# State-space outputs and gate kept as channels by tokens, the skip as a per-partition scalar, and the norm's root applied to the rows of the output projection

## The chip, the cores and the metric

The kernel runs on one core of a Trainium2 chip. The metric is the device time of one execution, in microseconds. Five engines work side by side, each through its own queue in order: PE (TensorE, matrix products into PSUM), DVE (VectorE), ACT (ScalarE), POOL (GpSimd) and SP (SyncE, which here issues the DMA transfers). PEld is the loading of a product's stationary operand.

## What is computed

One inference step of a one-layer trunk: 1024 prompt tokens and 8 streams of 16 decode tokens, width 1024. Three token mixers read the same normalised input: stick-breaking attention, a Mamba-2 state-space group (SSD) and forgetting attention (FoX). Cross-attention and a SwiGLU network follow. The change lies in the state-space group and in the projection that merges the three:

```python
proj = jnp.einsum('bnd,de->bne', u, p['w_in'])
sq, sk, sv, fq, fk, fv, fg, z, xbc, dt = split_last(proj, IN_SIZES)
...
xbc_c = jax.nn.silu(causal_dwconv(xbc_pad, p['conv_w'], p['conv_b']))
xs, Bm, Cm = split_last(xbc_c, (SSD_INNER, ...))
dt = jax.nn.softplus((dt + p['dt_bias']).astype(jnp.float32))
y, h_final = ssd_scan(xs * dt[..., None], dt * A, Bm, Cm, h0, ssd_chunk)
y = (y + p['d_skip'].astype(jnp.float32)[:, None] * xs).reshape(b, n, SSD_INNER)
ssd_o = rmsnorm(y * jax.nn.silu(z), p['ssd_norm_g'])      # over 512 channels
mix = jnp.concatenate([sb_o, fox_o, ssd_o], axis=-1)
out = jnp.einsum('bne,ed->bnd', mix, p['w_out'])
```

With y * silu(z) = s, the norm is s * g / sqrt(mean(s^2) + eps): the gain g belongs to a channel, the root to a token.

## The kernel before

All 1152 tokens stand in 9 blocks of 128; block 8 is the decode tokens. The normalised input is kept as channels by tokens (`uc`, three pieces of 384 tokens), each value as a high and a low part, so that a product of full precision is three products (`mm3`, lines 328 to 330).

**Two forms of projection.** `dense_T` keeps a weight tile stationary and streams 384 tokens: the result is 128 channels by 384 tokens. `dense_N` keeps 128 tokens stationary and streams up to 264 weight columns: the result is 128 tokens by channels. The convolution channels (`xbc_job`) come from `dense_T`, the gate (`z_proj`, `consume_z`) from `dense_N`, 256 columns at a time, with the 8 columns of dt beside its first half.

**The scan.** `ssd_gen` goes through the blocks in the order 8, 0, 1, ... 7, one chunk of 128 tokens each. For a chunk `load` fetches three things: the convolved channels, the decays broadcast to all partitions, and the gate. `prepare` transposes x and B to tokens by channels and makes the scaled forms of x (by dt, by the decay to the end, by the skip); `weights` makes the 128 by 128 decay weights of 8 heads; `states` multiplies C with the state (and for the decode block the streams' own states); `outputs` adds the heads' products, gates, squares with a sum over the row, and scales by the root and the gain; `write` transposes the 128 x 512 result to channels by tokens and stores it in `mix_sc`. The write of a chunk comes one chunk later, the last one in the `final` list.

**The order of the work.** A generator yields after each such step. The rows of both attentions are the main line; before each, the `fill` generator is advanced at the rate `RATE`: first the remaining projections in the order `ORD` (gate half 0, dt, convolution, gate half 1), then the scan. What is left is woven with the first half of the output projection (`heads_out`, `add_rows`: the attention channels), which adds 18 blocks of 128 x 512 into the residual rows `h`. Then `finish_rows` adds the state-space channels, again 18 products, from `mix_sc` by way of `load_unsplit`, which splits each value into high and low parts. The final place of each instruction on its engine is set by a scheduler that knows priorities and dependences.

**Buffers.** The scan's products take the 2 PSUM buffers `psd`, which the projections use too; the chunk's tiles A and B come from 6 big buffers `act`. DMA goes through SP's queue in order: a transfer that must wait for something holds all that is behind it.

Of the kernel before, what the change touches and what calls it, by code (L numbers as in the profile page):

```python
# [8 lines left out]
F32 = mybir.dt.float32  # L9
# [44 lines left out]
RATE = (1.0, 1.1, 60)  # L54
# [8 lines left out]
def tile_hybrid_step(ctx: ExitStack, tc: tile.TileContext, a: dict):  # L63
# [80 lines left out]
    SP.dma_start(out=rows[40:72, :P], in_=a["conv_w"][0].rearrange("i (k p) -> (i k) p", p=P))  # L144
    first_raw = []
# [73 lines left out]
    PE.transpose(colp[:, :72], rows[:72, :P], ident[:72, :72])  # L219
    cols = cst.tile([P, 72], F32, name="cols")  # L220
    DVE.tensor_copy(cols, colp[:, :72])
    DVE.tensor_scalar(cols[:, 32:72], cols[:, 32:72], 0.5, None, ALU.mult)
# [262 lines left out]
    def proj_v(m, c0, pv, sv, extra=0):  # L485
# [7 lines left out]
        return dense_N([(w_in, c0, 256 + extra)], blocks_of(uc), consume)  # L493
# [243 lines left out]
    def xbc_job(j):  # L737
# [9 lines left out]
        def consume(c, ps):  # L747
# [27 lines left out]
            SP.dma_start(out=xbc_sc[j * P:(j + 1) * P, 0:SEQ], in_=y)  # L775
            SP.dma_start(out=xbc_sc[j * P:(j + 1) * P, SEQ:T], in_=ysm[:, :P])
# [190 lines left out]
    def ssd_gen():  # L967
        sc = act_t(F32)
        hT, gB = sc[:, 0:512], sc[:, 512:1024]
# [65 lines left out]
        def load(i):  # L1035
            A = act_t(F32)
            SP.dma_start(out=A[:, 0:1024].rearrange("p (j t) -> p j t", t=P),
                         in_=xbc_sc[:, i * P:(i + 1) * P].rearrange("(j p) t -> p j t", p=P))
            SP.dma_start(out=A[:, 1024:2048],
                         in_=ac_sc[8 * i:8 * i + 8, :].rearrange("h t -> (h t)").unsqueeze(0).to_broadcast([P, 1024]))  # L1040
            SP.dma_start(out=A[:, 2048:2560], in_=z_sc[i * P:(i + 1) * P, :])
            return A

        def views(A, B):
# [4 lines left out]
        def prepare(i, A, B):
            xT, br, zt, Bn, cb, xn, xd, xe, xD = views(A, B)  # L1050
# [11 lines left out]
            heads_tt(xD, xn, ndsk)  # L1062

        def weights(i, A, B):
            xT, br, zt, Bn, cb, xn, xd, xe, xD = views(A, B)

            ps = pd()
            for g in range(2):
# [19 lines left out]
        def states(i, A, B, t1):  # L1088
            xT, br, zt, Bn, cb, xn, xd, xe, xD = views(A, B)
            hs = slice(8 * i, 8 * i + 8)  # L1090
            if i < 8:
                ps = pd()
                for g in range(2):
                    PE.matmul(ps[:, g * 256:(g + 1) * 256], xT[:, 6 + g, :], hT[:, g * 256:(g + 1) * 256],
                              start=True, stop=True)
                DVE.tensor_tensor(out=h3(t1), in0=h3(ps), in1=bc(ea[:, hs]), op=ALU.mult)
# [68 lines left out]
        def write(i, t1):  # L1165
            ps = pd()
            for j in range(4):
                PE.transpose(ps[:, j * P:(j + 1) * P], t1[:, j * P:(j + 1) * P], ident)
# [897 lines left out]
```

## Time and profile before

| | us |
|---|---|
| median of 3 runs | 1887.22 (1886.44 to 1888.09) |
| profiled execution | 1894.55 |
| its span, first to last instruction | 1892.8 |
| PE busy | 1837.7 (97%) |
| DVE busy | 886.4 (47%) |
| ACT busy | 802.1 (42%) |
| POOL busy | 617.9 (33%) |
| DMA, q1's share of 16 engines | 49.6% |

Lines of the page and of the trace name the line of the kernel, the engine, the operation and the tiles (output<-inputs), and how often. Busy times of matmuls overlap, so what a matmul costs PE is read from the distance between starts in the timeline. In brackets stands how long an engine was idle before an instruction and what released it; "issue" is idle time that nothing in the profile explains. Granted clock 1.00 is TensorE's full speed.

### The profile page before, as it was taken

The page shows a single profiled execution, that of the slowest core. Times are in us where ns is not written, and L with a number is a line of the kernel's source. Part 1 is how long each engine was busy: PE and PEld are TensorE (multiplying, and loading weights), DVE is VectorE, ACT ScalarE, POOL GpSimd, SP SyncE. Part 2 cuts the span into 40 slices and gives each one's busy share as a digit, 9 for nine tenths or more (in the row PEclk, how much of TensorE's full clock was granted, in tenths as well). Part 3 has the DMA queues.
Part 4 walks back from the last instruction along what each step waited for, and adds up shares of the span by engine and source line. Part 5 has one row for each costly group of instructions (what it writes and reads, how often), then busy time and mean ns, then how long its engine had stood idle before and what let it go on. Part 6 is the DMA issues. An engine that isn't in the chain of part 4 may idle for free.

```text
span 1892.8 us, 32368 instructions
## 1 busy us (share of the span) xinstructions
PE 1837.7 (97%) x12136; PEld 1638.6 (87%) x12136; DVE 886.4 (47%) x1798; ACT 802.1 (42%) x1719; POOL 617.9 (33%) x921
## 2 busy tenths in 40 slices
PE   7999999999999989999999989999999999999998
PEld 5899778888967767899988889999999999888886
DVE  3412323475656863444444586333333333455554
ACT  6522544545455862344332374333333333344443
POOL 7622425445115673111112107444444542000000
PEclk9999999999989999999999999999999999999999
DMA  9465654437587883245576124233322223657572
GB/s 338 145 189 149 206 142 133 147 109 207 179 249 228 282 290 102 108 134 173 173 271 219 56 81 112 75 87 79 76 71 70 70 70 105 207 187 243 174 243 89
DMA packets 291068, 296.64 MB, mean 157 GB/s; under 512 B 80092, under 2 KB 242884, under 8 KB 290912
## 3 DMA queue, kind: packets, MB, share of 16 engines
q1 hardware_dynamic: 290912, 294.57, 49.6%
q8 instruction: 96, 1.57, 0.3%
q14 instruction: 60, 0.49, 0.1%
HBM read 225.12 MB, written 69.91 MB: 156 GB/s over the span
## 4 chain that ended last, share of the span: by engine, by line
PE 83%; DMA 5%; DVE 4%; POOL 3%; ACT 3%; issue 2%; SPq 0%; DVEq 0%; POOLq 0%; ACTq 0%
PE psd L1868 11%; PE psd L328 10%; PE psd L329 10%; PE psd L330 10%; PE pst L1868 8%; PE pss L1868 4%; PE pss L328 3%; PE pss L330 3%; PE pss L329 3%; PE pso L1868 2%; POOL wl L132 2%; PE pst L328 1%; PE pst L329 1%; PE pst L330 1%; PE pso L593 1%
## 5 line engine op out<-in xcount | busy, mean ns | idle before, releaser
L132 POOL TENSOR_TENSOR wl<-wr,wh 128x256 fp32r<-128x256 f32 (+2 forms) x184 | 142.1, 805 | 233.0 <-ACT wh L292 232.8
L328 PE MATMUL psd<-act,wh 128*128 128x384 f32 x528 | 182.3, 345 | 0.0
L330 PE MATMUL psd<-act,wl 128*128 128x384 f32 x528 | 181.1, 343 | 0.6 <-POOL wl L132 0.6
L329 PE MATMUL psd<-act,wh 128*128 128x384 f32 x528 | 181.7, 344 | 0.0
L1868 PE MATMUL pst<-bT,tr 128*128 128x256 f32 (+1 forms) x1068 | 155.0, 293 | 0.0
L1868 PEld LDWEIGHTS pst<-bT,tr 128*128 128x128 f32 x1068 | 144.9, 188 | 0.1
L330 PE MATMUL psd<-wh,act 128*128 128x512 f32 (+3 forms) x424 | 136.9, 324 | 0.0
L329 PE MATMUL psd<-wl,act 128*128 128x256 f32 (+3 forms) x414 | 134.2, 325 | 2.7 <-POOL wl L132 2.7
L328 PE MATMUL psd<-wh,act 128*128 128x256 f32 (+3 forms) x414 | 133.3, 326 | 1.4 <-DMA act<-osc 1.0
L1868 PE MATMUL psd<-bT,tr 128*128 128x320 f32 (+1 forms) x912 | 132.8, 295 | 0.7 <-POOL tr L132 0.7
L1868 PEld LDWEIGHTS psd<-bT,tr 128*128 128x128 f32 x912 | 124.7, 188 | 1.0 <-POOL tr L132 0.9
L132 POOL TENSOR_TENSOR tr<-u,tr 128x256 fp32r<-128x256 f32 x110 | 82.6, 779 | 101.7 <-ACT tr L1704 83.8
L253 POOL TENSOR_SCALAR sm<-sm 128x1 f32<-128x1 f32 (+2 forms) x27 | 9.1, 338 | 297.3 <-ACT y L1970 207.8
L1843 DVE TENSOR_TENSOR tr<-tr,pst 128x256 f32<-128x256 f32 (+1 forms) x86 | 38.6, 449 | 139.9 <-ACT tr L1840 106.6
L330 PEld LDWEIGHTS psd<-act,wl 128*128 128x128 f32 x528 | 99.2, 188 | 3.2 <-issue 1.9
L132 POOL TENSOR_TENSOR ws<-ws 128x256 f32<-128x256 f32 (+2 forms) x100 | 69.3, 721 | 98.1 <-DVE ws L522 83.9
L328 PEld LDWEIGHTS psd<-act,wh 128*128 128x128 f32 x528 | 99.4, 188 | 2.2 <-issue 1.8
L329 PEld LDWEIGHTS psd<-act,wh 128*128 128x128 f32 x528 | 99.3, 188 | 1.9 <-issue 1.5
L132 POOL TENSOR_TENSOR tr<-raw,tr 128x256 fp32r<-128x256 f32 x94 | 69.2, 765 | 83.9 <-ACT tr L1704 75.7
L1704 ACT CAST tr<-tr 128x384 fp32r<-128x384 f32 (+1 forms) x70 | 37.6, 538 | 123.0 <-DMA tr<-hidsc 117.3
L329 PEld LDWEIGHTS psd<-wl,act 128*128 128x128 f32 x414 | 79.2, 191 | 10.9 <-POOL wl L132 4.0
L292 ACT CAST wh<-wr 128x512 fp32r<-128x512 f32 (+2 forms) x90 | 52.5, 622 | 81.7 <-PE psd L330 32.0
(643 smaller groups left out, 4730.5 us busy)
## 6 DMA issues: line engine op xcount, KB each, us to landing
u<-w_down SPq DMA_DIRECT2D x40, 512.0 KB
raw<-w_down SPq DMA_DIRECT2D x26, 512.0 KB
st<-qksc SPq DMA_DIRECT2D x48, 256.0 KB
wr<-w_in SPq DMA_DIRECT2D x44, 256.0 KB
tr<-hidsc SPq DMA_DIRECT2D x57, 192.0 KB
hidsc<-tr SPq DMA_DIRECT2D x34, 288.0 KB
qksc<-sg SPq DMA_DIRECT2D x48, 192.0 KB
wr<-cache_sb_k SPq DMA_DIRECT2D x32, 256.0 KB
```

The costliest lines, as they stand in the source:

```text
L132: POOL.tensor_tensor(out=out[:, a0:a1], in0=in0[:, a0:a1], in1=in1[:, a0:a1], op=op)
L253: POOL.tensor_scalar(v, ss, inv, EPS, ALU.mult, ALU.add)
L292: ACT.copy(hi, raw)
L328: PE.matmul(out, ah, bh, start=start, stop=False)
L329: PE.matmul(out, ah, bl, start=False, stop=False)
L330: PE.matmul(out, al, bh, start=False, stop=stop)
L593: return PE.matmul(po[r:r + 64, q_], vt[:, 2 * (k0 + i) + j, :], pfs[i][:, sl], start=start and k0 == 0 and (j == 0 or qp > 0), stop=k0 + ...
L1704: ACT.copy(hi, src)
L1843: DVE.tensor_tensor(out=at(out, g), in0=at(x, g), in1=ps[g][:, :GW[g]], op=op)
L1868: PE.matmul(dst[g][:, :GW[g]], x[:, ka], y[:, k, :], start=start and k == 0 and m == 0, stop=stop and k == 3 and m == 2, skip_group_check= ...
```

## The change

- The gate is projected by `dense_T`, 4 weight tiles by 3 pieces, and stored as channels by tokens behind the convolved channels, in one tensor `xbz_sc`. One transfer fetches both for a chunk, the z rows after the x, B and C rows. The dt columns move to the value projection of the first attention.
- The products of `states` and `outputs` swap their operands, so that results are channels by tokens. In `outputs` each head has a 64-wide stationary operand; two heads go to the two halves of the array's columns, one after the other in the order (`together`). The decay of C times the state, a column per token before, is now a row: two exponentials per chunk, on 64 partitions each, from the broadcast decays. The decode chunk's part is still made as tokens by channels and transposed.
- The skip is a scalar per partition: four multiply-adds on DVE on 128 x 128 pieces in place of two products and a sum on POOL.
- The gated result is stored at once. The squares go to PE (`sums`): a product with a matrix of ones, 32 columns wide, for each of 4 channel groups, on four quarters of the array; the four rows of sums go to `ss_sc`. The transposes, the copy, the root and the scaling of each chunk are gone.
- The gain (halved) is applied by `load_unsplit` as a scalar per partition, in four steps in place of two. The root is made once for all 9 blocks from `ss_sc`, read back as 128 partitions by 36 single values, and `finish_rows` multiplies each product by it while adding.
- `RATE[0]` goes from 1.0 to 0.912, since the gate yields 12 steps in place of 18 (62 in all in place of 68). The third number of `RATE` was not used.

```diff
-RATE = (1.0, 1.1, 60)
+RATE = (0.912, 1.1)
...
-        return dense_N([(w_in, c0, 256 + extra)], blocks_of(uc), consume)
+            else:
+                DVE.tensor_tensor(out=dts[:, blk, :], in0=ps[:, 256:264], in1=hb[:, 4:12], op=ALU.add)
+        return dense_N([(w_in, c0, 256 + extra)] + [(w_in, C_DT, 8)] * (not extra), blocks_of(uc), consume)
...
-    def consume_z(n):
-        def f(blk, ps):
-            t, zt = sg2_t(), sg_t()
-            gate(zt[:, :256], ps[:, :256], t, 0.5)
-            SP.dma_start(out=z_sc[blk * P:(blk + 1) * P, n * 256:(n + 1) * 256], in_=zt[:, :256])
...
+    def consume_z(j):
+        def f(c, ps):
+            zt = sg_t()[:, :CW]
+            gate(zt, ps, zt, 0.5)
+            SP.dma_start(out=xbz_sc[D + j * P:D + (j + 1) * P, c * CW:(c + 1) * CW], in_=zt)
...
     def z_proj(n):
-        yield from dense_N([(w_in, C_Z + 256 * n, 256)] + [(w_in, C_DT, 8)] * (n == 0), blocks_of(uc), consume_z(n))
+        for j in (2 * n, 2 * n + 1):
+            yield from dense_T(w_in, uc, [(C_Z + j * P, consume_z(j))])
...
         def load(i):
             A = act_t(F32)
-            SP.dma_start(out=A[:, 0:1024].rearrange("p (j t) -> p j t", t=P),
-                         in_=xbc_sc[:, i * P:(i + 1) * P].rearrange("(j p) t -> p j t", p=P))
-            SP.dma_start(out=A[:, 1024:2048],
+            SP.dma_start(out=A[:, 0:1536].rearrange("p (j t) -> p j t", t=P),
+                         in_=xbz_sc[:, i * P:(i + 1) * P].rearrange("(j p) t -> p j t", p=P))
+            SP.dma_start(out=A[:, 1536:2560],
                          in_=ac_sc[8 * i:8 * i + 8, :].rearrange("h t -> (h t)").unsqueeze(0).to_broadcast([P, 1024]))
-            SP.dma_start(out=A[:, 2048:2560], in_=z_sc[i * P:(i + 1) * P, :])
...
-            heads_tt(xD, xn, ndsk)
...
+            if i < 8:
+                for e in range(2):
+                    r = slice(64 * e, 64 * e + 64)
+                    ACT.activation(A[r, 2560:3072].rearrange("p (j t) -> p j t", t=P),
+                                   br.rearrange("p (j e t) -> p e j t", e=2, t=P)[r, e], AF.Exp)
...
-                for g in range(2):
-                    PE.matmul(ps[:, g * 256:(g + 1) * 256], xT[:, 6 + g, :], hT[:, g * 256:(g + 1) * 256],
-                              start=True, stop=True)
-                DVE.tensor_tensor(out=h3(t1), in0=h3(ps), in1=bc(ea[:, hs]), op=ALU.mult)
+                for j in range(4):
+                    PE.matmul(ps[:, j * P:(j + 1) * P], hT[:, j * P:(j + 1) * P], xT[:, 6 + j // 2, :], start=True, stop=True)
+                DVE.tensor_tensor(out=t1, in0=ps, in1=A[:, 2560:3072], op=ALU.mult)
...
-            pool_tt(t1, t1, xD, ALU.add)
+            for j in range(4):
+                sl = slice(j * P, (j + 1) * P)
+                DVE.scalar_tensor_tensor(t1[:, sl], xT[:, j, :], dsk[:, j:j + 1], (t1 if i < 8 else ps)[:, sl],
+                                         ALU.mult, ALU.add)
...
-            for h in range(8):
-                PE.matmul(ps[:, h * 64:(h + 1) * 64], br[:, h * P:(h + 1) * P], xd[:, h * 64:(h + 1) * 64],
-                          start=True, stop=True)
+            together([lambda j=j, e=e: PE.matmul(
+                ps[64 * e:64 * e + 64, j * P:(j + 1) * P], xd[:, (2 * j + e) * 64:(2 * j + e + 1) * 64],
+                br[:, (2 * j + e) * P:(2 * j + e + 1) * P], start=True, stop=True) for j in range(4) for e in range(2)])
             DVE.tensor_tensor(out=t1, in0=t1, in1=ps, op=ALU.add)
             pool_tt(t1, t1, zt, ALU.mult)
-            ss = small(1)
-            ACT.activation(xD, t1, AF.Square, accum_out=ss)
-            r = rstd_of(ss, 1, 1.0 / 2048)
-            DVE.scalar_tensor_tensor(t1, t1, r, gB, ALU.mult, ALU.mult)
...
+            ACT.activation(sq, t1, AF.Square)
+
+        def sums(i, A, B):
+            sq = views(A, B)[-1]
+            ps = pd()
+            together([lambda j=j: PE.matmul(ps[32 * j:32 * j + 32, :P], ones[:, 0:32], sq[:, j * P:(j + 1) * P],
+                                            start=True, stop=True) for j in (3, 0, 1, 2)])
+            ss = sg2_t()[:, :P]
+            ACT.copy(ss, ps[:, :P])
+            SP.dma_start(out=ss_sc[:, i * P:(i + 1) * P], in_=ss[0:P:32, :])
...
-                    DVE.tensor_tensor(out=h[blk][:, sl], in0=h[blk][:, sl], in1=ps, op=ALU.add)
+                    if scale is None:
+                        DVE.tensor_tensor(out=h[blk][:, sl], in0=h[blk][:, sl], in1=ps, op=ALU.add)
+                    else:
+                        DVE.scalar_tensor_tensor(h[blk][:, sl], ps, scale[:, blk:blk + 1], h[blk][:, sl], ALU.mult, ALU.add)
...
+    ssq = dts.rearrange("p a b -> p (a b)")
+    SP.dma_start(out=ssq[:, :4 * NBLK].rearrange("p (j b) -> p j b", j=4), in_=ss_sc.rearrange("j (b p) -> p j b", p=P))
+    sums2 = small(NBLK)
+    DVE.tensor_reduce(out=sums2, in_=ssq[:, :4 * NBLK].rearrange("p (j b) -> p b j", j=4), op=ALU.add, axis=AX)
+    r_ssd = ssq[:, 4 * NBLK:5 * NBLK]
+    DVE.tensor_copy(r_ssd, rstd_of(sums2, NBLK, 1.0 / 2048))
```

Three places show how instructions move. On SP, where the scan starts, before (`xbcsc` the convolved channels, `zsc` the gate, `acsc` the decays, `cache_fox` and `state_ssm` the decode streams' data):

```order
L1037 DMA act<-xbcsc 128x8x128
L882 DMA wr<-cache_fox_k 128x512
L1178 DMA act<-state_ssm 128x4x128 x2
L798 DMA zsc<-sg 128x256
L606 DMA mixsc<-so 64x256
L1178 DMA act<-state_ssm 128x4x128
L882 DMA wr<-cache_fox_k 128x512
L1178 DMA act<-state_ssm 128x4x128
L798 DMA zsc<-sg 128x256
...
```

and now:

```order
L945 DMA vr<-cache_fox_v 128x1024 x4
L610 DMA mixsc<-so 64x256
L802 DMA xbzsc<-sg 128x384 x2
L511 DMA st<-qksc 64x1024
L512 DMA st<-qksc 64x1024
L1040 DMA act<-xbzsc 128x12x128
L1192 DMA act<-state_ssm 128x4x128 x5
L610 DMA mixsc<-so 64x256
L1020 DMA acsc<-so 72x128
L1192 DMA act<-state_ssm 128x4x128 x3
L1042 DMA act<-acsc 128x1024
```

The first chunk's load stood ahead of the last gate stores, with the state loads among them; now it and all state loads stand behind the last gate store.

On PE, around one chunk's head products (L1156 before, L1168 now), before:

```order
L1156 MATMUL psd<-act 128x64 x8
L1168 MATMUL psd<-ident,sg 128x128 x4
L956 MATMUL pst<-fold_157,so 128x64
L578 MATMUL pst<-ident,ws 128x128 x7
L1069 MATMUL psd<-act 128x128 x2
```

and now, with the sums in L1181:

```order
L1168 MATMUL psd<-act 64x128 x8
L1070 MATMUL psd<-act 128x128 x2
L582 MATMUL pst<-ident,ws 128x128 x3
L597 MATMUL pso<-pt,st 64x256
L597 MATMUL pso<-pt,st 64x128
L891 MATMUL pst<-ident,wr 128x128 x12
L597 MATMUL pso<-pt,st 64x256 x3
L597 MATMUL pso<-pt,st 64x128
L891 MATMUL pst<-ident,wr 128x128 x4
L1181 MATMUL psd<-act 32x128 x4
```

The chunk before's transposes are gone, and the chunk's own sums follow after some of the attention's transposes and products.

On DVE, in the first half of the output projection now (L1332 adds a product of `add_rows`, which frees its PSUM buffer; L1425 reduces the sums, L257 to L1427 finish the root):

```order
L1332 TENSOR_TENSOR xc<-xc,psd 128x512
L1425 TENSOR_REDUCE sm<-dts 128x9
L1332 TENSOR_TENSOR st<-st,psd 128x512
L257 SCALAR_TENSOR_TENSOR sm<-sm 128x9
L1332 TENSOR_TENSOR st<-st,pss 128x512
L258 TENSOR_TENSOR sm<-sm 128x9
L1332 TENSOR_TENSOR st<-st,psd 128x512
L1332 TENSOR_TENSOR st<-st,pss 128x512
L259 SCALAR_TENSOR_TENSOR sm<-sm 128x9
L1427 COPY dts<-sm 128x9
```

Before, nothing but additions stood here; now the reduction, and with it everything behind it on the engine, waits for the sums to be read back.

More of the change, by code (lines that the diff above doesn't have):

```diff
@@ L144, in tile_hybrid_step @@
     SP.dma_start(out=rows[40:72, :P], in_=a["conv_w"][0].rearrange("i (k p) -> (i k) p", p=P))
+    SP.dma_start(out=rows[72:76, :P], in_=a["ssd_norm_g"].rearrange("o (k p) -> (o k) p", p=P))
     first_raw = []
@@ L218, in tile_hybrid_step @@
     colp = pT()
[L219 to L222, printed above, removed]
+    PE.transpose(colp[:, :76], rows[:76, :P], ident[:76, :76])
+    cols = cst.tile([P, 76], F32, name="cols")
+    DVE.tensor_copy(cols, colp[:, :76])
+    DVE.tensor_scalar(cols[:, 32:76], cols[:, 32:76], 0.5, None, ALU.mult)
     g_mix, g_x, g_ffn, g_mem = (cols[:, 8 * i:8 * i + 8] for i in range(4))
-    conv_b = cols[:, 32:40]
-    hb = mcst.tile([P, 28], F32, name="hb")
+    conv_b, g_ssd = cols[:, 32:40], cols[:, 72:76]
+    hb = mcst.tile([P, 24], F32, name="hb")
     lf = mcst.tile([P, NBLK, 4], F32, name="lf")
     dts = mcst.tile([P, NBLK, 8], F32, name="dts")
+    dsk = hb[:, 20:24]
     def dram(shape, dt, name):
@@ L968, in ssd_gen @@
         sc = act_t(F32)
[L969 removed]
+        hT = sc[:, 0:512]
         triu, btri, ones, bones = (sc[:, 1024 + 128 * i:1152 + 128 * i] for i in range(4))
@@ L1148, in states @@
                     yield
-                DVE.tensor_tensor(out=h3(t1), in0=h3(yo), in1=bc(ea[:, hs]), op=ALU.mult)
-            pool_tt(t1, t1, xD, ALU.add)
+                yn = sg_t()
+                DVE.tensor_tensor(out=h3(yn), in0=h3(yo), in1=bc(ea[:, hs]), op=ALU.mult)
+                ps = pd()
+                for j in range(4):
+                    PE.transpose(ps[:, j * P:(j + 1) * P], yn[:, j * P:(j + 1) * P], ident)
+            for j in range(4):
+                sl = slice(j * P, (j + 1) * P)
+                DVE.scalar_tensor_tensor(t1[:, sl], xT[:, j, :], dsk[:, j:j + 1], (t1 if i < 8 else ps)[:, sl],
+                                         ALU.mult, ALU.add)
@@ L1158, in outputs @@
             DVE.tensor_tensor(out=t1, in0=t1, in1=ps, op=ALU.add)
             pool_tt(t1, t1, zt, ALU.mult)
-            ss = small(1)
-            ACT.activation(xD, t1, AF.Square, accum_out=ss)
-            r = rstd_of(ss, 1, 1.0 / 2048)
-            DVE.scalar_tensor_tensor(t1, t1, r, gB, ALU.mult, ALU.mult)
[L1165 to L1168, printed above, removed]
-            ACT.copy(t1, ps)
@@ L1174, in ssd_gen @@
+        order = [8, 0, 1, 2, 3, 4, 5, 6, 7]
         A, nxt = load(order[0]), None
@@ L1201, in ssd_gen @@
             yield
-            if last:
-                write(*last)
-                yield
-            last = (i, t1)
             if n == 8:
-                final.append(lambda: write(i, t1))
+                final.append(lambda: sums(i, A, B))
             if n < 8:
@@ L1210, in ssd_gen @@
                 weights(order[n + 1], A1, B1)
+                yield
+                sums(i, A, B)
                 yield
@@ L1331, in pair_of, with finish_rows @@
         return [t(F32R) for _ in range(2)]
-    def finish_rows(w, k0, rows, h, homes, after, n):
+    def finish_rows(w, k0, rows, h, homes, after, n, scale=None):
         units = [[w_unit([(w, j * 512, 512)], k0 + k, 2, pair=pair and pair_of(pair), eng=eng)
@@ L1386, in load_unsplit @@
         SP.dma_start(out=f32(t[:, 1]), in_=src[k0:k0 + 4, :, c * CW:(c + 1) * CW].rearrange("k p t -> p k t"))
-        for k in (0, 2):
-            hi, lo = (t[:, x, k:k + 2] for x in range(2))
-            ACT.copy(hi, f32(lo))
-            DVE.tensor_tensor(out=lo, in0=f32(lo), in1=f32(hi), op=ALU.subtract)
+        for k in range(4):
+            hi, lo = (t[:, x, k] for x in range(2))
+            ACT.activation(hi, f32(lo), AF.Copy, scale=g_ssd[:, k:k + 1])
+            DVE.scalar_tensor_tensor(lo, f32(lo), g_ssd[:, k:k + 1], f32(hi), ALU.mult, ALU.subtract)
     def chunk_rows(ch):
```

31 lines of the change are left out of this document (14 added, 17 removed).

## The prediction

> **What bounds the kernel now.** I read the page's busy shares first, then a table of windows over the scan, then the timeline there.
>
> ```profile
> PE 1837.7 (97%) x12136; PEld 1638.6 (87%) x12136; DVE 886.4 (47%) x1798; ACT 802.1 (42%) x1719; POOL 617.9 (33%) x921
> ```
>
> TensorE has work nearly all the time. A matmul's busy time overlaps the next one's, so below I cost by distances between starts. The columns of the windows are length, then PE, PEld, DVE, ACT and POOL busy (instructions), the granted clock, the DMA share and GB/s.
>
> ```profile
> 515.00:545.00 30.00, 28.02 (x226) 21.68 (x225) 12.30 (x44) 15.90 (x41) 5.67 (x11) 1.00 0.97 308
> 545.00:600.00 55.00, 51.86 (x352) 35.56 (x351) 33.39 (x102) 28.07 (x61) 18.32 (x33) 0.81 0.76 242
> 600.00:660.00 60.00, 58.51 (x542) 46.59 (x541) 47.67 (x144) 44.94 (x110) 37.92 (x61) 1.00 0.73 246
> 660.00:700.00 40.00, 36.02 (x253) 26.64 (x251) 31.47 (x79) 27.46 (x55) 26.31 (x40) 1.00 0.84 291
> 720.00:780.00 60.00, 60.00 (x266) 48.51 (x265) 18.88 (x30) 13.81 (x24) 17.86 (x26) 1.00 0.31 106
> ```
>
> The scan runs beside the attention from about 515 to 700 us. PE lacks 2.0 + 3.1 + 1.5 + 4.0 = 10.6 us of 185 there, no other engine is near full, and DMA is full at the start. So PE work removed in this stretch should mostly come off the time. In 720 to 780, the output projection, PE never pauses: there only a new wait can count.
>
> **The change part by part.** The gate projection first.
>
> ```profile
> 520.46 0.28 PE L328 MATMUL psd<-wh,act 128*128 128x256 f32 x1
> 522.22 0.28 PE L328 MATMUL psd<-wh,act 128*128 128x256 f32 x1
> 424.37 0.34 PE L329 MATMUL psd<-act,wh 128*128 128x384 f32 x1
> 426.67 0.33 PE L330 MATMUL psd<-act,wl 128*128 128x384 f32 x1
> ```
>
> The 256-wide pair is 15 starts apart (0.117 us each), the 384-wide pair 13 (0.177). Before, the gate takes 216 matmuls of 264 and 216 of 256 columns: 216 x 0.121 (0.117 x 264 / 256) + 216 x 0.117 = 51.4 us. After, 4 x 3 x 24 = 288 of 384: 51.0. The dt columns widen 216 value matmuls by 8: +0.8. Together +0.4 us; layout alone saves nothing.
>
> Now one chunk of the scan.
>
> ```profile
> 652.97 2.00 PE L1156 MATMUL psd<-act 128*128 128x64 f32 x16
> 654.80 0.61 PE L1168 MATMUL psd<-ident,sg 128*128 128x128 f32 x4
> 655.25 0.33 PE L956 MATMUL pst<-fold,so 128*128 128x64 f32 x2
> 665.60 1.90 PE L1156 MATMUL psd<-act 128*128 128x64 f32 x16
> 667.31 0.48 PE L560 MATMUL pss<-st 128*128 128x512 f32 x1
> 648.16 1.08 PE L593 MATMUL pso<-pt,st 128*64 128x256 f32 x8
> 649.17 0.33 PE L924 MATMUL pst<-ident,ws 128*128 128x128 f32 x1
> 684.81 0.43 PE L902 MATMUL pss<-st,act 128*32 128x128 f32 x8
> 685.16 0.71 PE L1069 MATMUL psd<-act 128*128 128x128 f32 x4
> 656.97 1.03 PE L1094 MATMUL psd<-act 128*128 128x256 f32 x4
> 657.93 0.86 PE L593 MATMUL pso<-pt,st 128*64 128x256 f32 x4
> ```
>
> Eight heads' products (L1156, two passes each) take 1.83 and 1.71 us, mean 1.77: 0.11 a pass for only 64 columns. Transposed, each pass has 128 columns and a 64-wide stationary half, two halves side by side: 16 passes of 128, as much streaming as L593's 8 of 256 in halves, 1.01 us. Saving 0.76 x 9 chunks = 6.8. Bounds: none, if the halves don't overlap; 8.0, if they overlap perfectly (0.885).
> The write's four transposes (0.45) go: -4.05; the last chunk, the decode one, gets four back: +0.45. The sums of squares are four quarter-wide products, L902's form: 0.35 x 9 = +3.15. The product with the state becomes 8 passes of 128 for 4 of 256 (0.96): 8 x 0.11 = 0.9, taken as no change. PE in all: 0.4 - 6.8 - 4.05 + 0.45 + 3.15 = **-6.9 us**.
>
> L593 and L902 themselves show what changing the array's split costs: four passes of 256 at full width take 0.96, so eight in halves would take 0.96, against 1.01; a quarter of 8 x 0.11 is 0.22, against 0.35. The Trainium skill (TensorEngine Tiling, Key Properties) says that a change of tiling mode drains TensorE, which speaks against a change that adds two such groups to every chunk; the same page promises up to 2 and 4 times. By its full factors the sum would be 1.1 + 1.2 us lower, by the rows it is as above; the trace agrees with the drain, at about 0.05 to 0.13 us a group.
>
> Waits removed with the write:
>
> ```profile
> PEld psd L1168 <- ACT kf L890: 1.8, 1, 1.8
> PEld psd L1168 <- DVE st L1321: 1.7, 1, 1.7
> ```
>
> The transposes stalled PE for 3.5 us in all. The sums stand where they stood, need a PSUM buffer likewise, and additionally the square from ScalarE; I take half, **-1.7** (bounds -3.5 and 0).
>
> The other engines. Per chunk POOL loses two head products, the skip add and the root's steps; VectorE gets four skip multiply-adds for one scaling and three small steps; ScalarE gets two exponentials of 64 x 512 and a small copy for a copy and an accumulator read.
>
> ```profile
> L132 POOL TENSOR_TENSOR sg<-sg,act 128x256 f32<-128x256 f32 x36 | 27.5, 783 | 45.6 <-issue 26.4 <-DVE sg L1158 14.8 <-DVE sg L1096 2.8
> L772 DVE SCALAR_TENSOR_TENSOR sg<-sg,cols 128x128 f32<-128x128 f32 x24 | 10.4, 433 | 0.0
> L1082 ACT ACTIVATE act<-act 128x384 f32<-128x384 f32 (+1 forms) x18 | 11.0, 628 | 3.1 <-DVE act L1079 3.1
> ```
>
> POOL saves half of the 27.5 us and more. VectorE: 4 x 0.43 = 1.7, about 1.2 removed. ScalarE: 2 x 0.63 = 1.26 added, about 0.6 net. PE's attention work covers these, at 35% to 75% load; if the cover were gone, ScalarE's would cost 5 us over eight chunks (a rival below). The exponentials read the decays that VectorE then overwrites, so VectorE's subtractions, and the attention rows queued behind them, wait for ScalarE.
>
> The scan's start. Now one load brings convolution and gate channels together, so the first chunk's waits until the last gate piece has landed, and on SP's queue the state loads are behind it. Before, that load went out while the second half of the gate was still being computed.
>
> ```profile
> 513.82 0.37 SPq L1037 DMA_DIRECT2D act<-xbcsc  x1
> 523.55 0.29 POOL L1111 COPY act<-act 128x128 f32<-128x128 f32 x1 [10.55 <-DMA act<-xbcsc]
> 521.19 0.40 ACT L418 ACTIVATE so<-psd 128x256 f32<-128x256 f32 x1
> 521.63 0.42 DVE L419 SCALAR_TENSOR_TENSOR sg<-so,psd 128x256 f32<-128x256 f32 x1 [0.65 <-ACT so L418]
> 537.76 0.35 SPq L1017 DMA_DIRECT2D acsc<-so  x1
> 540.73 0.32 SPq L1039 DMA_DIRECT2D act<-acsc  x1
> 526.05 0.33 PE L1001 MATMUL psd<-act 128*128 128x64 f32 x2
> 527.91 0.30 PE L888 MATMUL pst<-ident,wr 128*128 128x128 f32 x1
> ```
>
> From the last gate matmul: gate 0.9, store landed 3.0 (540.73 - 537.76, where SP waited for it), then the load: at least another 3, at most the 9.7 us that it took before with the DMA full. That is 6.9 to 13.6. In the new order PE has, between that matmul and the first transposes, attention scores of 5504 columns (2.5 us at the rate below), one L593 group (1.0), the decay sums (1.9) and a transpose (0.3): 5.7. Stall 1.2 to 7.9, less the 2.0 that PE idles there already: -0.8 to 5.9. DMA is near full in that window, but its bulk is the same; I take the middle, **+2.6**.
>
> The root. It is applied when VectorE adds the projection, and needs all sums.
>
> ```profile
> DMA packets 746, 0.02 MB, mean 47 GB/s; under 512 B 736, under 2 KB 746, under 8 KB 746
> q1 hardware_dynamic: 746, 0.02, 88.1%
> 716.36 0.39 PE L328 MATMUL psd<-wh,ws 128*128 128x512 f32 x1
> 718.23 0.39 PE L330 MATMUL psd<-wh,ws 128*128 128x512 f32 x1
> ```
>
> They come back as 4608 elements of 4 bytes. The first two rows are DMA in 277.5 to 278.0 us, nearly all small packets: 16 engines x 0.5 us x 0.881 / 746 = 9.4 ns each, so 4608 / 16 x 9.4 ns = 2.7 us. From the last sum: copy 0.5, store 3.0, load 3.0 + 2.7, reduction 0.2 = 9.4 us. On VectorE the reduction stands ahead of the additions that free PSUM; PE's order has 36 matmuls until it needs the first of these buffers, 36 x 0.234 (8 starts, 716.36 to 718.23) = 8.4. **+0.9** (bounds 0, and 5 if weight loads double the DMA's part).
>
> Sum: -6.9 - 1.7 + 2.6 + 0.9 = -5.1 us. The profiled execution took 1894.55 (span 1892.8), so 1889.5 for it; the median of the runs is 1887.2, 0.4% less, and with the same difference **1882.1**.
>
> **The rivals.**
> *Slower by the scan's start.* The first load decides: from some 10 us after the last gate matmul on. Stall 5.9, and the first state transposes wait for 1 MB behind it (3.4 us at 308 GB/s, about 1 covered: +2.4). A pause there can halve the clock:
>
> ```profile
> 560.00:570.00 10.00, 10.00 (x36) 4.60 (x35) 5.25 (x16) 3.83 (x7) 0.82 (x2) 0.50 0.76 223
> 620.00:630.00 10.00, 9.82 (x69) 7.89 (x68) 8.41 (x24) 9.95 (x24) 7.81 (x16) 1.00 0.60 206
> ```
>
> Ten microseconds at 0.50, as already in the first row, lose 5. Sum -8.6 + 0.9 + 5.9 + 2.4 + 5.0 = +5.6: 1892.8. For it: SP issues in order. Against: the scheduler put attention work into the gap. The Trainium skill (TensorE: Matmul & The Clock Gate, Part 1) has an idle window of about 3.4 us lower the clock to half; the row agrees with the half, not with how it comes about.
> *ScalarE becomes the scan's bound.* The second row has it at 9.95 of 10. If the added 0.6 a chunk lies ahead of what PE waits for, 8 x 0.6 = +4.8 beside the -5.1: 1886.9, no change.
> *More than forecast.* No stall at the start and the 2.0 idle there gone, all 3.5 of the write's waits gone, no gate: -6.9 - 3.5 - 2.0 = -12.4: 1874.8.
> *The halves don't run side by side:* +6.8 beside the -5.1: 1888.9. L593 speaks against it.
>
> **How the numbers follow.** Forecast 0.44, slower start 0.25, ScalarE 0.17, more 0.11, no overlap 0.03. A change under 0.2% (3.8 us) can't be told from none here. The forecast's own spread, 1879 to 1886, is faster in 0.32, same in 0.11, slower in 0.01; the start slower 0.21, same 0.04; ScalarE same 0.12, slower 0.03, faster 0.02; more, faster 0.11; the last same 0.02, slower 0.01. So faster 0.45, same 0.29, slower 0.26. The range runs from the best case to beyond the slow one, since unlisted shifts of the order add a little: 1873 to 1895.
>
> **What would show it.** The eight-head group near 1.0 us for 16 passes, the sums near 0.35, no ident transposes of the chunk outputs; PE's idle time at the scan's start 5 us, not 2; the reduction's wait on the sums' load, with PE pausing about a microsecond in the projection. Wrong: a head group above 1.5 us, idle time above 8 us at the start, or PE waiting on ScalarE's exponentials in each chunk.

## The result and the profile after

The changed kernel takes **1907.14 us** (median of 6 runs, 1898.38 to 1914.18) against 1887.65 us before, a ratio of 1.0101 (95% interval 1.0074 to 1.0128). Forecast was 1882.1 in a range of 1873 to 1895: a small gain, and it is a loss of 19.5 us. The profiled execution took 1904.89.

First the page's busy shares and the span with the mean granted clock, of the changed kernel, and the same clock row of the kernel before.

```profile
PE 1835.2 (96%) x12064; PEld 1636.0 (86%) x12064; DVE 885.8 (47%) x1803; ACT 809.9 (43%) x1725; POOL 583.1 (31%) x869
```
```profile
core 0: 1903.2 us, clock 0.984
```
```profile
core 0: 1892.8 us, clock 0.988
```

Two things can be read off. TensorE's idle time (span less busy) went from 1892.8 - 1837.7 = 55.1 to 1903.2 - 1835.2 = 68.0 us, **+12.9**. And the granted clock fell. As a measure of what that costs I take span x (1 - clock), since every clock record of these two traces is full or half: 22.7 us in this run of the kernel before, 30.5 in that of the changed one. Each run lists its clock, so the same can be done for all of them: the changed kernel lost 31.4 us on average (21 to 38), the kernel before 16.1 (13 to 21, eleven runs of another round). Call what is left the time at full clock: 1875.3 against 1871.7. By this measure the 19 us are **+3.6 at full clock and +15.3 of half clock**. The profiled run of before (1894.55) had been one of those with more half clock than usual. One execution of a later kernel (g2 below) had a mean clock of 0.751 and took 2240.7 us; it is left out.

The measure is too high, because half clock that falls into a pause lengthens nothing. Taken as half of TensorE's busy time at half clock, the cost in the two profiled runs is 20.2 us where the clock records give 23.2 before, and 23.0 where they give 30.3 after. With it the two spans, 10.4 us apart, add up: +12.9 of idle time, +2.8 of half clock on the work, and -5.3 for the work itself. From run to run of one kernel the time rose by about 0.7 us for each us of the measure (180 executions of the kernels below, each kernel's mean taken out), so an estimate of what the 15.3 us really cost is 11.

Windows by stage, before and then after: from the first attention score to the scan's first product, and from there to the end of the output projection's attention half. Columns are length, PE, PEld, DVE, ACT, POOL busy, clock, DMA share, GB/s.

```profile
127.20:526.05 398.85, 383.78 (x2845) 344.85 (x2844) 173.33 (x313) 175.72 (x403) 148.99 (x236) 0.98 0.55 161
526.05:752.30 226.25, 215.30 (x1570) 162.25 (x1569) 142.55 (x393) 127.55 (x279) 106.24 (x169) 0.95 0.69 229
```
```profile
128.70:537.70 409.00, 391.41 (x2782) 348.57 (x2780) 178.17 (x322) 180.97 (x410) 146.02 (x232) 0.98 0.55 162
537.70:760.80 223.10, 202.46 (x1560) 150.95 (x1560) 135.78 (x391) 130.38 (x281) 75.16 (x118) 0.95 0.72 223
```

TensorE's idle time is length less busy: 15.1 and 10.9 us before, 17.6 and 20.6 after. The stretch with the scan has 9.7 of the 12.9 us. TensorE's timeline shows the longest pauses there, and three ahead of the forget gate's sums:

```profile
282.64 1.13 PE L927 MATMUL pst<-ident,ws 128*128 128x128 f32 x4 [5.40 <-POOL ws L132]
292.93 0.60 PE L686 MATMUL psd<-lf,sg 128*128 128x32 f32 x2 [3.12 <-DVE lf L662]
295.30 0.63 PE L687 MATMUL psd<-so,sg 128*128 128x28 f32 x2 [1.77 <-DVE so L684]
...
546.32 1.08 PE L1056 MATMUL psd<-ident,act 128*128 128x128 f32 x4 [2.82 <-DMA act<-xbzsc]
...
617.09 0.99 PE L1056 MATMUL psd<-ident,act 128*128 128x128 f32 x4 [3.65 <-DMA act<-xbzsc]
...
630.00 0.43 PE L1181 MATMUL psd<-act 128*32 128x128 f32 x8 [1.79 <-ACT act L1175]
632.87 1.62 PE L1106 MATMUL psd<-act 128*128 128x256 f32 x3 [0.88 <-DVE sg L1102]
```

And the clock in windows laid around such places, all about half:

```profile
279.00:286.50 7.50, 3.86 (x18) 3.58 (x18) 4.44 (x8) 2.35 (x9) 7.50 (x10) 0.54 0.76 196
292.50:303.50 11.00, 8.48 (x37) 6.96 (x38) 5.71 (x17) 3.81 (x10) 6.26 (x10) 0.53 0.44 105
...
617.00:620.60 3.60, 3.51 (x16) 3.35 (x17) 0.95 (x3) 1.57 (x4) 0.00 (x0) 0.53 1.11 256
630.50:638.00 7.50, 6.62 (x30) 5.61 (x32) 2.85 (x7) 4.52 (x12) 2.71 (x5) 0.54 0.64 206
```

A pause can thus be paid twice: in its own length, and in half clock on the work beside it. The work itself came out as forecast. TensorE's order in one chunk, changed kernel:

```profile
642.28 0.42 PE L1181 MATMUL psd<-act 128*32 128x128 f32 x8
642.64 1.16 PE L1101 MATMUL psd<-act 128*128 128x128 f32 x8
643.73 1.93 PE L876 MATMUL pss<-kf,act 128*32 128x512 f32 x16
...
652.66 1.09 PE L1168 MATMUL psd<-act 128*64 128x128 f32 x16
653.69 1.23 PE L927 MATMUL pst<-ident,ws 128*128 128x128 f32 x8
```

By distances between starts the head products take 1.03 us (1.77 before), the sums of squares 0.36, the state's product 1.09.

### The profile page after: what moved, and what is told of

It reads as the page before. It is cut to its first block, busy times and chain, and to the rows that moved or that the text cites. A ratio compares the mean times of both kernels' runs of the same rounds, so it can differ in the third digit from the quotient of the medians.

```text
span 1903.2 us, 32145 instructions
## 1 busy us (share of the span) xinstructions
PE 1835.2 (96%) x12064; PEld 1636.0 (86%) x12064; DVE 885.8 (47%) x1803; ACT 809.9 (43%) x1725; POOL 583.1 (31%) x869
## 4 chain that ended last, share of the span: by engine, by line
PE 81%; DMA 8%; DVE 4%; POOL 2%; ACT 2%; issue 2%; SPq 1%; DVEq 0%; POOLq 0%; ACTq 0%
PE psd L1888 11%; PE psd L332 9%; PE psd L330 9%; PE psd L331 9%; PE pst L1888 8%; PE pss L1888 4%; PE pss L330 3%; PE pss L331 3%; PE pss L332 3%; PE pso L1888 2%; PE pso L597 2%; PE pst L582 2%; PE pst L330 2%; PE pst L331 2%; PE pst L332 2%
## 5 line engine op out<-in xcount | busy, mean ns | idle before, releaser
L330 PE MATMUL psd<-act,wh 128*128 128x384 f32 x624 | 214.9, 345 | 0.5 <-DVE sg L458 0.5
L332 PE MATMUL psd<-act,wl 128*128 128x384 f32 x624 | 214.6, 344 | 0.0
L331 PE MATMUL psd<-act,wh 128*128 128x384 f32 x624 | 214.1, 343 | 0.0
L132 POOL TENSOR_TENSOR wl<-wr,wh 128x256 fp32r<-128x256 f32 (+1 forms) x184 | 136.0, 775 | 235.4 <-ACT wh L294 233.4
L332 PEld LDWEIGHTS psd<-act,wl 128*128 128x128 f32 x624 | 117.2, 188 | 3.2 <-issue 2.9
L330 PEld LDWEIGHTS psd<-act,wh 128*128 128x128 f32 x624 | 117.5, 188 | 2.4 <-issue 0.9
L331 PEld LDWEIGHTS psd<-act,wh 128*128 128x128 f32 x624 | 117.3, 188 | 2.3 <-issue 1.9
L255 POOL TENSOR_SCALAR sm<-sm 128x1 f32<-128x1 f32 (+3 forms) x19 | 5.5, 287 | 298.2 <-ACT y L1990 209.0
L332 PE MATMUL psd<-wh,act 128*128 128x512 f32 (+2 forms) x280 | 95.6, 343 | 0.0
L330 PE MATMUL psd<-wh,act 128*128 128x512 f32 (+2 forms) x270 | 91.9, 346 | 1.9 <-ACT wh L294 1.1
L331 PE MATMUL psd<-wl,act 128*128 128x512 f32 (+2 forms) x270 | 92.1, 343 | 0.0
L1860 ACT COPY tr<-psd 128x320 f32<-128x320 f32 (+1 forms) x105 | 42.1, 401 | 97.2 <-PE psd L1888 97.1
L1724 ACT CAST tr<-u 128x512 fp32r<-128x512 f32 x128 | 75.4, 619 | 17.8 <-PE pst L1888 3.4
```

The lines of the kernel that those rows point to most:

```text
L132: POOL.tensor_tensor(out=out[:, a0:a1], in0=in0[:, a0:a1], in1=in1[:, a0:a1], op=op)
L255: POOL.tensor_scalar(v, ss, inv, EPS, ALU.mult, ALU.add)
L330: PE.matmul(out, ah, bh, start=start, stop=False)
L331: PE.matmul(out, ah, bl, start=False, stop=False)
L332: PE.matmul(out, al, bh, start=False, stop=stop)
L1724: ACT.copy(hi, src)
```

## The experiments

Time at full clock and loss to the half clock are means over a kernel's runs by the measure above, which puts too much on the half clock; the ratio is to the kernel before on the same chip, whose median was 1886.8 to 1890.1 in the rounds below (the first row is one of them). "Idle" is TensorE's, in the profiled run, from the scan's first product to the end of the output projection's attention half. The pace is `RATE[0]`, projection steps to an attention unit.

| kernel | pace | median | ratio (95%) | full clock | half-clock loss | idle in the scan |
|---|---|---|---|---|---|---|
| before | 1.0 | 1887.8 | 1 | 1871.7 | 16.1 | 10.9 |
| before, scan step rate 1.05 (h1) | 1.0 | 1889.3 | 1.0017 (1.0002 to 1.0033) | 1872.4 | 18.6 | 11.5 |
| before, scan step rate 1.2 (h2) | 1.0 | 1896.6 | 1.0043 (1.0030 to 1.0056) | 1874.6 | 20.7 | 17.1 |
| before (f4) | 1.02 | 1897.6 | 1.0045 (1.0027 to 1.0063) | 1872.6 | 25.0 | 18.8 |
| before (e8) | 0.95 | 1896.7 | 1.0043 (1.0028 to 1.0058) | 1871.9 | 23.9 | 22.0 |
| before (e1) | 0.912 | 1911.5 | 1.0121 (1.0096 to 1.0147) | 1881.9 | 28.6 | 19.8 |
| changed | 0.912 | 1907.1 | 1.0101 (1.0074 to 1.0128) | 1875.3 | 31.4 | 20.6 |
| changed (e2) | 1.0 | 1913.8 | 1.0145 (1.0127 to 1.0164) | 1884.5 | 30.6 | 33.6 |
| changed (g1) | 0.97 | 1902.0 | 1.0065 (1.0043 to 1.0087) | 1876.7 | 25.7 | 23.8 |
| changed (g2) | 0.93 | 1908.1 | 1.0093 (1.0061 to 1.0125) | 1875.5 | 31.2 | - |
| changed (e7) | 0.95 | 1896.3 | 1.0043 (1.0030 to 1.0057) | 1874.7 | 21.2 | 23.2 |
| changed, scan step rate 1.2 (g3) | 0.95 | 1903.9 | 1.0077 (1.0049 to 1.0105) | 1876.7 | 27.8 | 25.4 |
| store late (e3) | 0.912 | 1901.0 | 1.0069 (1.0052 to 1.0085) | 1878.0 | 22.8 | 19.6 |
| gate apart (e4) | 0.912 | 1902.5 | 1.0088 (1.0070 to 1.0105) | 1876.2 | 27.9 | 21.6 |
| both (e5) | 0.912 | 1907.1 | 1.0105 (1.0090 to 1.0120) | 1876.6 | 30.5 | 22.2 |
| both (e6) | 0.95 | 1904.1 | 1.0096 (1.0074 to 1.0117) | 1880.3 | 25.5 | 28.7 |
| store late (g4) | 0.95 | 1902.4 | 1.0060 (1.0037 to 1.0082) | 1875.9 | 26.0 | 22.6 |
| before, heads twice (f1) | 1.0 | 1908.3 | 1.0103 (1.0080 to 1.0126) | 1891.2 | 17.2 | 14.0 |
| changed, heads twice (f2) | 0.95 | 1907.9 | 1.0099 (1.0081 to 1.0117) | 1882.6 | 25.3 | 23.2 |
| changed, no exponentials (f3) | 0.95 | 1900.0 | 1.0057 (1.0036 to 1.0078) | 1877.7 | 22.2 | 26.4 |

An interval reaches some 3 to 5 us to either side, so smaller differences say nothing. Sums of single waits below are worked out from the gaps of the trace between the same two points.

### The pace alone, put in and taken out

The kernel before with the changed one's pace, and the changed kernel with that of before:

```diff
-RATE = (1.0, 1.1, 60)
+RATE = (0.912, 1.1)
```
```diff
-RATE = (0.912, 1.1)
+RATE = (1.0, 1.1)
```

> The kernel before with one number of the change alone: the pace at which projection steps are put between the attention units, 0.912 in place of 1.0. Theory P (the new pace moves the forget gate's sums to a place where TensorE waits for them: 10.3 us in three gaps at 282 to 295 us of the changed kernel, against 1.8 us there before, partly made up at 200 to 276): 1890 to 1893 us, with those gaps in its trace. Theory Q (all of the loss is the scan's loads): 1887.6, no change.

> The changed kernel with the pace of before, 1.0. Theory P: 3 to 6 us better than the changed kernel's 1907.1, so 1901 to 1904, and the gaps at 282 to 295 shrink to a few us. Theory Q: 1907, the gaps in the scan stay.

Measured: 1911.5 and 1913.8. Neither theory has this. The pace alone makes the kernel before as slow as the whole change made it, and taking it back makes the changed kernel no faster. In e1's timeline the pauses at the sums are much like those of the changed kernel (5.40, 3.12 and 1.77 there):

```profile
280.83 1.13 PE L924 MATMUL pst<-ident,ws 128*128 128x128 f32 x4 [2.33 <-POOL ws L132]
284.01 1.13 PE L924 MATMUL pst<-ident,ws 128*128 128x128 f32 x4 [2.05 <-POOL ws L132]
...
294.60 0.61 PE L682 MATMUL psd<-lf,sg 128*128 128x32 f32 x2 [2.82 <-DVE lf L658]
296.62 0.63 PE L683 MATMUL psd<-so,sg 128*128 128x28 f32 x2 [1.41 <-DVE so L680]
```

So these belong to the pace, not to the layout: at 0.912 the sums stand behind 346 rows of attention work in TensorE's order, in both kernels, against 257 at 1.0. But the pace also moves the scan. In e1 it starts at 552.6 us in place of 526.1, behind more of the attention, and its windows show the idle time on both sides (423.90 - 404.84 = 19.1 and 207.90 - 188.14 = 19.8 us, against 15.1 and 10.9):

```profile
128.70:552.60 423.90, 404.84 (x3049) 360.25 (x3048) 191.40 (x363) 190.47 (x436) 145.97 (x243) 0.97 0.56 165
552.60:760.50 207.90, 188.14 (x1362) 145.03 (x1361) 131.90 (x342) 110.67 (x245) 103.21 (x158) 0.98 0.66 217
```

In e2 the wait on GpSimd ahead of the sums is down to 1.17 us. Others came, 4.21 us on a load of the attention nearby, and several where the scan and the attention meet, the longest on a GpSimd step of the attention:

```profile
540.28 1.93 PE L876 MATMUL pss<-kf,act 128*32 128x512 f32 x8 [5.26 <-POOL act L872]
...
547.95 1.94 PE L891 MATMUL pst<-ident,wr 128*128 128x128 f32 x8 [2.00 <-DMA wr<-cache_fox_k]
```

### The two waits on the scan's loads

SP's queue in the changed kernel shows how the 3.65 us at 617 us came about: the outputs' store waits for GpSimd's gating, and the load of the chunk after next stands behind it.

```profile
600.31 0.49 SPq L610 DMA_DIRECT2D mixsc<-so  x1
607.12 0.38 SPq L1173 DMA_DIRECT2D mixsc<-sg  x1
607.59 1.00 SPq L1040 DMA_DIRECT2D act<-xbzsc  x1
```

Before, the store at this place was that of the chunk ahead, long finished. Edits: the store behind the load (e3); the gate in a tensor and a load of its own (e4); both (e5); both at the pace 0.95 (e6).

```diff
             if n < 8:
                 nxt = load(order[n + 2]) if n < 7 else None
+                store(i, t1)
```
```diff
-    xbz_sc = dram([D + 512, T], F32, "xbzsc")
+    xbz_sc = dram([D, T], F32, "xbzsc")
+    z_sc = dram([512, T], F32, "zsc")
...
+            SP.dma_start(out=A[:, 1024:1536].rearrange("p (j t) -> p j t", t=P),
+                         in_=z_sc[:, i * P:(i + 1) * P].rearrange("(j p) t -> p j t", p=P))
```

> The changed kernel with the store of a chunk's outputs issued behind the load of the chunk after next, no longer ahead of it. Theory Q (SP's queue holds the load back until VectorE and GpSimd have made the outputs): the 3.65 us wait on the loads at 617 us goes, and with it a half-clock stretch of 3.4 us (1.7 us lost): 1901 to 1903. Theory P: 1907, since the load is hidden or another wait takes over.

> The changed kernel with the gate channels in a scratch tensor of their own and loaded by a third load behind the decays, as before; the conv channels' load no longer waits for the last gate store. Theory Q: the 2.8 us gap at the scan's start (546 us) goes, with the half clock that follows it (6.8 us, 3.4 lost): 1901 to 1903. Theory P, or if the extra queue entries cost as much: 1907.

> The changed kernel with both edits, the store behind the load and the gate channels loaded apart. Alone they gave 1901.0 and 1902.5, 6.1 and 4.6 us less than the 1907.1. Theory W (each wait has its own cause in the change and goes with it): 1896, and both gaps on the loads (546 and 617 us) are gone from one trace. Theory O (any new order of the scan meets as many waits somewhere else): 1900 to 1903, no better than one edit alone.

> Both edits, and the pace 0.95 in place of 0.912, at which the forget gate's sums stand behind 277 attention rows of TensorE's order (257 in the kernel before, 346 in the changed one) and the scan's first matmul behind 780 (796 and 855). Theory W: the 10.3 us of gaps at the sums shrink to some 3 and their half clock with them (8.5 us lost to 3): 1896 - 7 to 10 = 1886 to 1889, as fast as before. Theory O: 1895 to 1905.

Measured: 1901.0, 1902.5, 1907.1, 1904.1. Each edit did what it says to its wait: with e3 the load is issued ahead of the store and the wait at 617 us is gone, with e4 the one at 546 us, and in e5 TensorE never waits for these loads. Yet e5 is no faster than the changed kernel, and its idle time is the same:

```profile
537.80:762.00 224.20, 202.00 (x1560) 148.30 (x1560) 136.58 (x391) 129.29 (x281) 70.85 (x116) 0.93 0.69 218
```
```profile
617.13 0.43 PE L960 MATMUL pst<-fold,so 128*128 128x64 f32 x2 [2.65 <-DVE so L956]
...
671.09 1.11 PE L892 MATMUL pst<-ident,wr 128*128 128x128 f32 x4 [3.25 <-ACT kf L894]
...
710.70 0.54 PE L331 MATMUL psd<-wh,ws 128*128 128x512 f32 x1 [2.96 <-ACT ws L1392]
```

224.20 - 202.00 = 22.2 us. Summed over the scan's part of the trace, the waits of the scan's own steps fell from 12.8 (changed) to 3.9 us, and those of the attention's steps rose from 5.3 to 14.5. Theory W falls. Nor are waits on the scan's loads the change's own: TensorE waits 1.1 us for them in the kernel before and 6.5 in the changed one, but 5.3 and 6.2 in the kernel before at the paces 0.912 (e1) and 0.95 (e8). The gains of e3 and e4 alone, with intervals that touch that of the changed kernel, can't be put down to the waits they removed; at the pace 0.95 the edit of e3 even lost:

> The changed kernel at the pace 0.95 with the store of a chunk's outputs behind the load. At 0.912 this edit took 6.1 us off. If it removes a wait of its own: 1889 to 1893. If it was the new order that happened to fit: 1894 to 1905.

Measured: 1902.4, against 1896.3 without the edit, though TensorE's waits on the scan's loads went from 2.2 us to none. So at 0.912 it was the order that fitted, not the wait removed.

### The pace 0.95 in both kernels

> The changed kernel with the pace 0.95 alone. Theory W: the sums' gaps go, the scan's stay: 1897 to 1900. Theory O: 1900 to 1915, the pace 1.0 gave 1913.8.

> The kernel before with the pace 0.95 (the sums behind 277 attention rows, the scan behind 890). Theory W: most of the 23.7 us that the pace 0.912 cost lies at the sums, so 1890 to 1895. Theory O (the kernel before stands at a pace that fits its order, and each other pace costs 10 us or more): 1898 to 1910.

The edit is the same number again. Measured: 1896.3 and 1896.7, the same time for both kernels. For the changed one it is the best found, 10.8 us better than its own pace, and it loses 5 us more to the half clock than the kernel before, where its own pace lost 15 more; at the sums it has one pause of 3.98 us in place of three. For the kernel before it is a loss of 9 us. By the measure that is nearly all half clock (1871.9 at full clock against 1871.7), but e8's trace has 9 us more idle time than that of before (64.1 against 55.1), so the measure doesn't part the two here.

### Does TensorE's work still count?

If removing waits only moves them, TensorE may not be the bound at all. The head products computed twice:

```diff
-            for h in range(8):
+            for h in [*range(8), *range(8)]:
```
```diff
-                br[:, (2 * j + e) * P:(2 * j + e + 1) * P], start=True, stop=True) for j in range(4) for e in range(2)])
+                br[:, (2 * j + e) * P:(2 * j + e + 1) * P], start=True, stop=True) for _ in range(2) for j in range(4) for e in range(2)])
```

> The kernel before with every chunk's eight head products computed twice, 1.77 us more of TensorE work a chunk, 15.9 in all; the output is the same. Theory T (TensorE's work sets the scan's length, as the prediction took it): 1887.8 + 15.9 = 1904. Theory C (the chains through DMA, ScalarE and VectorE set it, and TensorE's work and idle time trade for each other): under 1896, with less idle time in the scan than 11 us.

> The changed kernel at the pace 0.95 (1896.3 us) with the head products computed twice, 1.0 us more of TensorE work a chunk, 9.1 in all. Theory T: 1905. Theory C: 1894 to 1899, idle time in the scan some 9 us below the 23 us of the run without.

Measured: 1908.3 and 1907.9. At full clock that is +19.5 us for 15.9 of added work, and +7.9 for 9.1. The windows of f2, and of e7 without the extra work ahead of it:

```profile
516.90:751.40 234.50, 211.31 (x1662) 153.25 (x1661) 142.95 (x405) 137.44 (x297) 75.25 (x118) 0.97 0.73 232
```
```profile
517.80:761.60 243.80, 220.56 (x1806) 163.71 (x1805) 139.12 (x405) 137.60 (x297) 72.67 (x118) 0.96 0.71 224
```

The stretch is 9.3 us longer, and the idle time is 23.2 us in both. Theory T holds: added work doesn't fill the pauses, and work removed doesn't vanish into them. The pauses stand beside it.

### ScalarE

```diff
-                    ACT.activation(A[r, 2560:3072].rearrange("p (j t) -> p j t", t=P),
-                                   br.rearrange("p (j e t) -> p e j t", e=2, t=P)[r, e], AF.Exp)
...
-                DVE.tensor_tensor(out=t1, in0=ps, in1=A[:, 2560:3072], op=ALU.mult)
+                DVE.tensor_tensor(out=t1, in0=ps, in1=A[:, 0:512], op=ALU.mult)
```

> The changed kernel at the pace 0.95 with the change's two exponentials a chunk left out (the state's product is multiplied by other data instead, so the outputs of the scan are not the reference's): 10 us less of ScalarE work in the scan. If ScalarE bounds the scan (the rival of the prediction): 1886 to 1890, and TensorE's waits on ScalarE (5.8 us in the scan's steps) mostly gone. If it does not, or the wait goes elsewhere: 1894 to 1899.

Measured: 1900.0, not faster. The 10 us of ScalarE work were not in the way, and in the other eleven traces of the changed program no wait of TensorE ends with these exponentials. What grew in this run is the sums' wait for the squares, five pauses of 7.1 us in all, such as this one:

```profile
628.01 0.42 PE L1176 MATMUL psd<-act 128*32 128x128 f32 x8 [2.35 <-ACT act L1170]
```

### Other orders of the same work

> The kernel before with the pace 1.02. Theory O (its order at 1.0 fits unusually well, and neighbours on both sides meet more waits): 1893 to 1905, like 0.95 with 1896.7. If the pace acts by the place of the forget gate's sums alone (here behind 257 attention rows as at 1.0): 1887 to 1890.

> The changed kernel with the pace 0.97: the forget gate's sums stand behind 257 attention rows of TensorE's order as in the kernel before, the scan's first matmul behind 773 (796 before). If the sums' place and the scan's place decide, 1893 to 1897, near 0.95's 1896.3. If each order brings its own waits, anywhere from 1893 to 1912 and not between its neighbours' 1896.3 (0.95) and 1913.8 (1.0).

> The changed kernel with the pace 0.93 (the sums behind 286 rows, the scan behind 838). If the sums' place decides: the 8.6 us of gaps before them shrink as at 0.95, 1896 to 1900. If each order brings its own waits: 1893 to 1912.

> The changed kernel at the pace 0.95, with 1.2 scan steps to an attention unit in place of 1.1. Only the order inside the scan changes. If the change's waits in the scan are its own, 1895 to 1898. If the order sets them: 5 us or more away from 1896.3, either way, and a chance for a version under 1887.

> The kernel before with 1.05 scan steps to an attention unit in place of 1.1; the scan starts at the same place and does the same work. If the order before is an unusually fitting one: 1893 to 1900, idle time in the scan nearer to 17 than to 9 us and some 8 us more lost to the half clock. If the scan of the kernel before meets few waits in any order: 1886 to 1890.

> The kernel before with 1.2 scan steps to an attention unit. The same two answers: 1893 to 1900, or 1886 to 1890.

All six change only numbers of `RATE`. Measured: 1897.6, 1902.0, 1908.1, 1903.9, 1889.3, 1896.6. Neither answer of h1 and h2 is the whole of it: at the pace 1.0 the scan of the kernel before keeps few pauses with the rate 1.05, and gets more with 1.2. The pace 1.02 costs it 9.8 us. The place of the sums doesn't decide: f4 and g1 have them behind 257 rows as before and are slow. No version beat the kernel before.

## Why the prediction failed

**The work on TensorE: right.** Head products -0.74 x 9 = -6.7 (forecast -6.8), the write's transposes gone, the sums 0.36 x 9 = +3.2 (+3.15). The state's product was taken as no change; it takes 1.09 for 0.96, +1.0 over eight chunks. In sum -5.7 for the forecast -6.9, and -5.3 by the account of the two profiled spans. That this work counts in full was only assumed; f1 and f2 show it.

**The root: right.** VectorE's reduction waited for the sums' load, and TensorE then paused for 0.56 us (forecast 0.9; its terms, 9.4 less 8.4, give 1.0):

```profile
746.10 0.22 DVE L1425 TENSOR_REDUCE sm<-dts 128x9 f32<-128x36 f32 x1 [7.94 <-DMA dts<-sssc]
```
```profile
746.98 0.50 PE L330 MATMUL psd<-wh,ws 128*128 128x512 f32 x1 [0.56 <-DVE st L1332]
```

**The scan's start: right in kind.** The pause on the combined load was there, 2.82 us (and 0.64 just before it) for the forecast stall of 1.2 to 7.9. Its consequence was not followed far enough: with e4 the pause went and another of 2.07 us came 7 us later, on the attention.

**"The sums stand where they stood": wrong.** The write worked on the chunk before, finished long ago; the sums work on the chunk just made, and follow its product, addition, gating and square through four engines. TensorE waited 2.6 us for the squares in the profiled run, and 0 to 7.1 in the other changed kernels, while the write's transposes waited 0 to 0.7 us in the other orders of the kernel before. The 3.5 us that the trace of before showed ahead of the write are waits of the weight loads; TensorE's matmuls waited 2.9 us there. They belonged to that one order, so the term of -1.7 had no ground; the change brings a wait here rather than removing one. The same slip hides in the store: moved forward by one chunk, it now waits in SP's queue ahead of a load. Both follow from the diff, from the line where `write(*last)` becomes `sums(i, A, B)`. Putting the sums off by one chunk was not tried.

**"Unlisted shifts of the order add a little": the step that failed.** The forecast kept the 10.6 us of idle time in the scan's stretch as given, up to two named terms. But that figure is a property of one order of the work. Every one of the twelve traces of the changed program has 19.6 to 33.6 us there, where the changed kernel itself has 20.6, and the kernel before has 17 to 22 in four of the other six of its traces. The change's pace number, which the prediction did not price at all, costs the kernel before 23.7 us by itself. Nor does it act alone: taken out again it costs the changed kernel more.

**A pause was priced at its own length: the second step that failed.** The half clock stood in one rival only (+5, for one place), and the row shown for it, at 560 us, has no pause in it (TensorE is busy for 10.00 of 10 us). By the measure it is 15.3 of the 19 us, by the estimate 11.

The rival of a slower start named the right mechanism for one of the pauses, and fell short in size. ScalarE as the bound is refuted by f3. That the halves don't overlap is refuted by the 1.03 us.

What stays open: why the changed scan has more pauses than the kernel before, 24.2 us on the mean of its twelve traces against 16.3 of seven, and 23.2 against 10.9 at a like place (scan behind 780 rows of attention in e7, 796 before). The waits for the squares and their copies explain 1.2 to 5.4 us of it in the runs with exponentials, the loads up to 6.5; with the loads' waits gone (e5) the rest came up elsewhere. At an equal pace the rest of the change is worth -4.4 us at 0.912 and -0.4 at 0.95, neither distinguishable from nothing, and +26 at 1.0, so it has no single price.

## What to carry to other kernels

Where a scheduler places several streams of work on one engine, treat the idle time of the tuned order as something that the change may lose, not as given: read from the diff which consumer moved closer to its producer, and what is queued behind it, and let the range reach as far as the same kernel moves when only a pacing number is turned. Price a pause on TensorE as its length plus half clock on the work behind it, and count the half clock only where TensorE is busy. And before a change is judged, time the kernel before with the change's own scheduling numbers.

## What was not expected of the hardware

Short pauses cost the clock, and which of them do depends on where they fall. In each of the 19 traces read (all but g2's), the half-clock stretches between 60 and 1880 us start on one grid of 3.413 us, to within 2 ns, and last one to six steps of it. A window of that grid in the changed kernel that is nearly all pause, and the one behind it (the clock is the third number from the end):

```profile
613.80:617.21 3.41, 0.12 (x1) 0.15 (x2) 0.37 (x3) 0.00 (x0) 0.00 (x0) 1.00 1.06 203
617.21:620.62 3.41, 3.41 (x16) 3.22 (x16) 0.97 (x3) 1.59 (x4) 0.00 (x0) 0.50 1.12 262
```

Counted over all windows of the grid in these traces, TensorE's idle time in a window against the clock in the next:

| idle in a window at full clock | windows | next one at half clock |
|---|---|---|
| under 1.25 us | 3677 | 6 |
| 1.25 to 1.75 us | 99 | 15 |
| 1.75 to 2 us | 48 | 42 |
| 2 us and more | 80 | 80 |

Behind a window already at half clock, 0.75 us of idle time was enough: the next one stayed at half in 48 of 48 cases, and in 43 of 132 with less. So a pause that is split between two windows can go free: of 71 pauses of 2 to 3 us, 13 had no half clock within 3 us, and all 13 left less than 2 us in any one window. And several short ones in one window can cost as much as a long one: in g3, pauses of 0.71, 0.65 and 0.71 us between 1130 and 1133.3 us are followed by half clock from 1133.4. A step at half clock costs at most 1.7 us, where TensorE is busy all through. The Trainium skill (TensorE: Matmul & The Clock Gate, HAM oscillation) puts the rule as no idle gaps above about 3.4 us; the counts here put the point lower, near 1.75 us within one window. This is a coincidence in time over many windows; no run set a pause on purpose. Nor is it the only cause: the longest stretch in the kernel before followed no pause above 0.3 us. Ten of the fourteen products in the window ahead of it use 32 of the array's 128 rows; whether that is the cause, no run tells.

```profile
556.00:576.60 20.60, 20.60 (x77) 12.77 (x75) 10.48 (x37) 10.45 (x21) 3.35 (x6) 0.50 0.70 204
```

The runs of one kernel spread with it: the fastest of the changed kernel (1898.38) had a clock of 0.989, the slowest (1914.18) 0.980, and 0.009 of 1905 us is 17 us, about what lies between them.
